# A first stage of block products: q and k of the band and B's gates are projected ahead of phase A and pass through DRAM

## The chip, the cores and the metric

The kernel runs on one core of a Trainium2 chip. The metric is the device time of one execution in microseconds (us). The two versions of the kernel are compared by the medians of several executions, and one execution of each is profiled.

The engines are TensorE (PE, with its weight loads PEld), VectorE (DVE), ScalarE (ACT), GpSimd (POOL) and SyncE (SP), which issues most of the loads. ACT issues most of the stores.

## The reference

The reference is one step of a hybrid encoder layer over 1024 prompt frames and 8 x 16 sample frames, 1152 columns in all, with a model width of 1024, all in float32:

```
z   = x @ w_in -> [q_A | k_A | v_A | q_B k_B v_B | q_C | gate logits (3*D) | a_B | b_B]
o_A = chunk-band softmax attention over the own chunk and the 8 before (16 heads of 64)
o_B = gated DeltaNet: causal conv + SiLU, normalised q/k, delta rule (8 heads of 128)
o_C = cross-attention into 256 memory tokens (4 heads of 256)
h   = LayerNorm(alpha * x + (sum_b sigmoid(gate_b) * o_b) @ w_out)
y   = LayerNorm(alpha * h + relu(h @ w_ff1 + b_ff1)^2 @ w_ff2 + b_ff2)
```

The keys and values of the band are outputs as well, among others.

## The kernel before

**Products.** A float32 product is made of three matmuls on halves: a matrix is split into `hi` (rounded to the type float32r) and `lo` (the rest), and hi\*hi, hi\*lo and lo\*hi are added in PSUM. x lies in SBUF transposed, as `xh` and `xl`, eight blocks of 128 rows by 1152 columns. The columns of `w_in` are cut into 80 tiles of 128: q of the band is tiles 0 to 7, k 8 to 15, v 16 to 23, the conv inputs of B 24 to 47, q of C 48 to 55, the gates of A, B and C 56 to 79. `projected` makes one tile: three chunks of 384 columns, for each 8 x 3 matmuls into one of two PSUM banks (tag `g`), and after each chunk an evacuation that its caller hands in. One tile is 72 matmuls of 384 columns.

**Seven products of eight.** `ffn1` already has another form for most of its tiles. It takes two tiles of the weights, the two halves of the inner dimension and the two halves of the columns as a 2 x 2 x 2 block product and makes it from seven products in place of eight, with sums of blocks (`S`, made once from the right-hand side, and `tsum`, made for each pair from the weights). Each product has two banks of 288 columns with 12 matmuls each, so a pair of tiles is 168 matmuls of 288 columns.

**Stages.** The stages are phase A (band attention, and the conv front of B), phase C, phase B (the delta rule), the output projection and the two FFN products. Each opens pools of SBUF and PSUM, and the next one's pools take the same places.

**Phase A.** At its start x is loaded and split, q and k of group 0 are projected as x arrives, `b_setup` prepares B, and `a_v(0)` projects v. Then there are eight groups g of two heads. A group is eight units `a_prompt` (256 query rows of one head: S on PE, softmax over DVE, ACT and POOL, transposes, split, product with v into `od`), `a_sample`, a gate tile of B, `b_front` (three conv tiles of B: conv, SiLU, transposes, stores to DRAM) and then `a_qk(g + 1)` and `a_v(g + 1)`.

**What sets the order.** Nobody writes the engines' orders out. A scheduler goes through the program by priority, which is the order of the program text, and puts an instruction on its engine as soon as its inputs and a buffer are there. So a projection fills PE's gaps in attention code that stands ahead of it in the text. A tile named with a tag shares that tag's few buffers: `y` has four (the conv's working tile, the v copies, a copy in `a_qk`), `qs0`, `qs1`, `kd0`, `kd1` and `vv` have one each, `tb` (tag `t`) has two, `od` one, the tag `f` for conv and v transposes one.

**B's gates** are eight tiles. Seven are projected in phase A (`b_gate(1, g)` for g < 7), and the eighth, (1, 7), stands in the list `gates`, which the later stages use as filling work. All eight are stored to DRAM in `gb` and read by phase B.

Of the kernel before, what the change touches and what calls it, by code (L numbers as in the profile page):

```python
# [63 lines left out]
class K:  # L64
# [66 lines left out]
    def setup(self):  # L131
# [93 lines left out]
    def load_x(self, pool):  # L225
# [3 lines left out]
        for c in range(NCH):  # L229
# [3 lines left out]
            for k in range(KT):  # L233
                xr = pool.tile([P, (CW, 640, CW, 3 + CW)[k % 4]], F32, name=("e", "pt", "y", "z")[k % 4], bufs=(2, 2, 4, 2)[k % 4])[:, 0:CW]
                self.xlast = nc.sync.dma_start(xr, xT[c, :, k, :]).ins.name
                self.split(self.xh[:, k, n], self.xl[:, k, n], xr, "act")


    def phase_a(self, keep, pool, ps):
        nc, d = self.nc, self.d  # L240
        self.A = A = {}
        self.load_x(pool)
# [27 lines left out]
        for g in range(8):  # L270
# [11 lines left out]
            if g < 7:  # L282
                self.a_qk(g + 1, pool)
                self.a_v(g + 1, pool, ps)

    def a_qk(self, g, pool):
# [21 lines left out]
        def ev_k(c, p):  # L308
# [959 lines left out]
    def ffn1(self, pool, ps, hm, raws):  # L1268
# [7 lines left out]
        one, two = slice(0, H), slice(H, NT)  # L1276
        top, low = slice(0, 4), slice(4, 8)

        S = {i: tuple(pool.tile([P, 4, H], F32R, name=f"s{i}{n}") for n in "hl") for i in (2, 1, 4)}
        S[3] = hh[:, top, two], hl[:, top, two]  # L1280
        names = cycle("gtogto")

        def bank():
            tag = next(names)
            if tag == "g":
                return self.psg.tile([P, 512], F32, name="ps", tag="g")[:, 0:288]
            return ps.tile([P, 512], F32, name=tag + "p", tag=tag, bufs={"t": 2, "o": 3}[tag])[:, 0:288]

        def hidden(r, f, i):
            nc.scalar.activation(r, r, AF.Relu, bias=bf[:, f:f + 1])  # L1290
            nc.scalar.activation(r, r, AF.Square)
            nc.scalar.dma_start(self.hid[f, i], r)

        res = lambda: pool.tile([P, H], F32, name="r", bufs=3)
        for f in range(4):
            w = self.weights(d["w_ff1"][f].rearrange("p (k c) -> p k c", k=KT))
            for i in range(2):
# [7 lines left out]
                nc.scalar.dma_start(self.hid[f, i], r)  # L1305
        for k in range(4):
# [9 lines left out]
        pool = self.on_right("p2r")  # L1316
        A11, A12, A22 = [(hh[:, q, n], hl[:, q, n]) for q, n in ((top, one), (low, one), (low, two))]
        for f in range(4, NF, 2):
            R = {}
            for g in range(2):  # L1320
                src = d["w_ff1"][f + g].rearrange("p (k c) -> p k c", k=KT)
                for q in range(2):
                    R[q, g] = raws().rearrange("p (k c) -> p k c", k=4)
                    nc.sync.dma_start(R[q, g], src[:, 4 * q:4 * q + 4, :])
            t1, t2, t3, t4 = (pool.tile([P, 4, P], F32, name="tsum", bufs=6) for _ in range(4))
            half = lambda j: slice(288 * j, 288 * j + 288)
            keep = lambda: pool.tile([P, H], F32, name="keep", bufs=5)
            def product(a, raw):

                w = [self.wp.tile([P, 4, P], F32R, name=n, tag=n, bufs=4) for n in ("whi", "wlo")]  # L1330
                self.split(*w, raw)
                banks = []
                for j in range(2):
                    banks.append(bank())
                    for k in range(4):
                        for m, (x, y) in enumerate(((0, 0), (0, 1), (1, 0))):
                            self.mm(banks[j], lhsT=w[x][:, k, :], rhs=a[y][:, k, half(j)], start=k == m == 0, stop=k == 3 and m == 2)
                return banks

            def add(x, banks):  # L1340
                y = keep()
                for j in range(2):
                    nc.vector.tensor_add(y[:, half(j)], banks[j], x[:, half(j)])  # L1343
                return y

            p1 = keep()
            for j, b in enumerate(product(A11, R[0, 0])):
                nc.scalar.copy(p1[:, half(j)], b)
            hidden(add(p1, product(A12, R[1, 0])), f, 0)
            nc.gpsimd.tensor_sub(t1, R[0, 1], R[0, 0])  # L1350
            nc.gpsimd.tensor_sub(t2, R[1, 1], t1)
            u2 = add(p1, product(S[2], t2))
            u4 = add(u2, product(S[1], t1))
            nc.gpsimd.tensor_sub(t4, R[1, 0], t2)
            u5 = add(u2, product(A22, t4))
            nc.gpsimd.tensor_sub(t3, R[1, 1], R[0, 1])
            hidden(add(u4, product(S[4], R[1, 1])), f + 1, 0)
            b = product(S[3], t3)
            hidden(add(u5, b), f, 1)
            hidden(add(u4, b), f + 1, 1)  # L1360

# [167 lines left out]
```

## Time and profile before

| | us |
|---|---|
| median of 3 runs (lowest, highest) | 2717.9 (2714.59, 2720.93) |
| the profiled execution, time | 2710.72 |
| the profiled execution, span from first to last instruction | 2708.9 |
| PE busy | 2607.6 (96%) |
| DVE busy | 1494.4 (55%) |
| ACT busy | 1063.6 (39%) |
| POOL busy | 866.9 (32%) |

An engine is busy while an instruction of its runs; issuing a DMA is not counted. Matmuls overlap their successors, so a PE that is busy all the time can still hold matmuls of different pace. The mean granted TensorE clock is 0.987 of full speed.

### The profile page before, as it was taken

The page shows a single profiled execution, that of the slowest core. Times are in us where ns is not written, and L with a number is a line of the kernel's source. Part 1 is how long each engine was busy: PE and PEld are TensorE (multiplying, and loading weights), DVE is VectorE, ACT ScalarE, POOL GpSimd, SP SyncE. Part 2 cuts the span into 40 slices and gives each one's busy share as a digit, 9 for nine tenths or more (in the row PEclk, how much of TensorE's full clock was granted, in tenths as well). Part 3 has the DMA queues.
Part 4 walks back from the last instruction along what each step waited for, and adds up shares of the span by engine and source line. Part 5 has one row for each costly group of instructions (what it writes and reads, how often), then busy time and mean ns, then how long its engine had stood idle before and what let it go on. Part 6 is the DMA issues. An engine that isn't in the chain of part 4 may idle for free.

```text
span 2708.9 us, 46387 instructions
## 1 busy us (share of the span) xinstructions
PE 2607.6 (96%) x16793; PEld 2418.9 (89%) x16793; DVE 1494.4 (55%) x3475; ACT 1063.6 (39%) x2851; POOL 866.9 (32%) x1203
## 2 busy tenths in 40 slices
PE   8999999999999989999989999999999998999998
PEld 7989999999999989888978888888899997878887
DVE  5647474756556573333466666554644445544545
ACT  5646474646556462232433333233622223101103
POOL 2222222222222221221555555332354442231112
PEclk9999999999999999999999999899999999999999
DMA  6343434444343444444776767554322224522311
GB/s 224 109 148 120 149 119 161 137 149 146 128 160 116 149 147 150 148 146 159 243 196 199 205 204 205 177 174 155 114 104 100 100 100 150 202 66 74 125 41 70
DMA packets 283782, 390.57 MB, mean 144 GB/s; under 512 B 57232, under 2 KB 189984, under 8 KB 280992
## 3 DMA queue, kind: packets, MB, share of 16 engines
q1 hardware_dynamic: 211344, 269.53, 31.7%
q10 hardware_dynamic: 72208, 118.06, 12.5%
q8 instruction: 133, 2.18, 0.3%
q14 instruction: 97, 0.79, 0.1%
HBM read 291.28 MB, written 128.72 MB: 155 GB/s over the span
## 4 chain that ended last, share of the span: by engine, by line
PE 78%; DMA 9%; DVE 6%; issue 3%; ACT 1%; POOL 1%; SPq 0%; DVEq 0%; ACTq 0%; POOLq 0%
PE ps L115 38%; PE op L115 19%; PE tp L115 4%; PE od L115 3%; PE S L115 3%; PE t L115 2%; PE tb L120 2%; PE sc L115 1%; DVE tmp L788 1%; PE tp L120 1%; PE kk L115 1%; DMA bv<-spn 1%; PE o L115 1%; DMA wraw<-in_w_mem 1%; DMA uraw<-hid 1%
## 5 line engine op out<-in xcount | busy, mean ns | idle before, releaser
L115 PE MATMUL ps<-xh,whi 128*128 128x384 f32 (+2 forms) x2144 | 749.0, 349 | 10.3 <-POOL whi L170 7.4
L115 PE MATMUL ps<-xh,wlo 128*128 128x384 f32 (+2 forms) x2144 | 726.7, 339 | 1.4 <-DVE wlo L171 1.4
L115 PE MATMUL ps<-xl,whi 128*128 128x384 f32 (+2 forms) x2144 | 725.8, 339 | 0.0
L115 PEld LDWEIGHTS ps<-xh,whi 128*128 128x128 f32 (+1 forms) x2144 | 404.2, 189 | 22.7 <-POOL whi L170 7.6
L115 PEld LDWEIGHTS ps<-xl,whi 128*128 128x128 f32 (+1 forms) x2144 | 404.4, 189 | 9.0 <-issue 5.0
L115 PEld LDWEIGHTS ps<-xh,wlo 128*128 128x128 f32 (+1 forms) x2144 | 403.5, 188 | 6.8 <-issue 2.5
L170 POOL TENSOR_SCALAR whi<-wraw 128x512 fp32r<-128x512 f32 x205 | 138.4, 676 | 441.6 <-PE ps L115 361.3
L115 PE MATMUL op<-l,xh 128*128 128x512 f32 x576 | 225.7, 392 | 8.0 <-DVE l L171 8.0
L115 PE MATMUL op<-h,xh 128*128 128x512 f32 x576 | 225.2, 394 | 8.3 <-POOL h L170 4.7
L115 PE MATMUL op<-h,xl 128*128 128x512 f32 x576 | 225.4, 391 | 0.0
L171 DVE TENSOR_TENSOR wlo<-wraw,whi 128x512 fp32r<-128x512 f32 x205 | 146.7, 717 | 137.4 <-POOL whi L170 134.1
L374 POOL TENSOR_SCALAR pt<-pt,sta 128x640 f32<-128x640 f32 (+3 forms) x144 | 110.9, 770 | 277.5 <-DVE sta L373 230.0
L166 ACT CAST xh<-uraw 128x384 fp32r<-128x384 f32 x96 | 45.5, 512 | 293.7 <-PE op L115 195.5
L620 DVE SCALAR_TENSOR_TENSOR y<-z,wc,y 128x384 f32<-128x384 f32 (+1 forms) x216 | 132.8, 615 | 28.4 <-ACT y L617 18.8
L170 POOL TENSOR_SCALAR h<-raw 128x512 fp32r<-128x512 f32 x64 | 54.3, 870 | 276.6 <-DVE acc L1412 168.0
L1412 DVE TENSOR_TENSOR acc<-op,acc 128x512 f32<-128x512 f32 x108 | 73.7, 688 | 117.4 <-PE op L115 117.4
L115 PEld LDWEIGHTS op<-h,xh 128*128 128x128 f32 x576 | 109.0, 189 | 33.0 <-POOL h L170 5.7
L115 PEld LDWEIGHTS op<-l,xh 128*128 128x128 f32 x576 | 109.1, 189 | 31.5 <-DVE l L171 8.7
L115 PEld LDWEIGHTS op<-h,xl 128*128 128x128 f32 x576 | 109.0, 189 | 22.7
L372 ACT ACTIVATE pt<-pt,sta 128x640 f32<-128x640 f32 (+3 forms) x144 | 101.0, 701 | 64.3 <-DVE sta L371 53.4
L1290 ACT ACTIVATE keep<-keep,bf 128x576 f32<-128x576 f32 x56 | 42.0, 774 | 211.2 <-DVE keep L1343 211.2
L370 DVE CUSTOM_DVE_ANT_0 pt<-S,tab 128x640 f32<-128x640 f32 (+4 forms) x128 | 83.8, 655 | 52.4 <-PE S L115 38.7
(473 smaller groups left out, 5971.7 us busy)
## 6 DMA issues: line engine op xcount, KB each, us to landing
wraw<-in_w_in SPq DMA_DIRECT2D x160, 256.0 KB
raw<-in_w_ff SPq DMA_DIRECT2D x120, 256.0 KB
uraw<-hid SPq DMA_DIRECT2D x32, 576.0 KB
kb<-in_cak SPq DMA_DIRECT2D x16, 1024.0 KB
vb<-in_cav SPq DMA_DIRECT2D x16, 1024.0 KB
hid<-keep ACTq DMA_DIRECT2D x56, 288.0 KB
o_aks<-in_cak ACTq DMA_DIRECT2D x32, 496.0 KB
o_avs<-in_cav ACTq DMA_DIRECT2D x32, 496.0 KB
```

The costliest lines, as they stand in the source:

```text
L115: ins = self.nc.tensor.matmul(out, **kw)
L120: ins = self.nc.tensor.transpose(out, **kw)
L166: nc.scalar.copy(hi, raw)
L170: nc.gpsimd.tensor_scalar(hi, raw, 1.0, 0.0, op0=ALU.mult, op1=ALU.add)
L171: nc.vector.tensor_sub(lo, raw, hi.bitcast(F32))
L370: nc.vector.tensor_tensor_reduce(out=P_, in0=S, in1=tab, scale=1.0, scalar=-3e38, op0=ALU.add, op1=ALU.max, accum_out=st[:, 0:1])
L372: nc.scalar.activation(P_, P_, AF.Exp, bias=st[:, 1:2], accum_out=st[:, 2:3])
L374: nc.gpsimd.tensor_scalar(P_, P_, st[:, 3:4], 0.0, op0=ALU.mult, op1=ALU.add)
L620: nc.vector.scalar_tensor_tensor(y[:, :w], z[:, i:i + w], wc[:, i:i + 1], y[:, :w], op0=ALU.mult, op1=ALU.add)
L788: nc.vector.tensor_tensor(tmp[:, 0:t, 0:t], y[:, 0:t, 0:t], m[:, 0:t, t].unsqueeze(1).broadcast_to([72, t, t]), op=ALU.mult)
L1290: nc.scalar.activation(r, r, AF.Relu, bias=bf[:, f:f + 1])
L1412: nc.vector.tensor_add(a, o, a)
```

## The change

A stage `phase_0` goes ahead of phase A, with pools of its own. It loads x into one large tile `xm`, projects q and k of groups 0 and 1 in the old way (tiles 0, 8, 1 and 9), makes the block sums of x, and then runs ten pairs through `seven`, the body of the loop of `ffn1` made into a function: six pairs (q, k) of groups 2 to 7 and four pairs of B's gates. The sixteen tiles of q and k go to a new DRAM array `zqk`, the gates to `gb` as before.

`a_qk` no longer projects. It loads six chunks of 128 x 384 from `zqk` into tiles of the tag `y` and hands them to the old evacuations, which now read SBUF. It stands ahead of `b_front(g)` in the text, no longer behind it. The gate tile leaves phase A's loop, and (1, 7) leaves the list `gates`. `seven` holds, for each pair, four weight loads, four sums of weights on POOL, seven products of 2 x 12 matmuls, fourteen evacuations and four calls of `out`; its text is the loop of `ffn1` shown above. `ffn1` calls the same new functions and computes what it did.

```
             self.right = st.enter_context(ExitStack())
+            with self.pools("0", "p0") as (pool, ps):
+                self.phase_0(pool, ps)
             with self.pools("a", "pa") as (pool, ps):
...
-        self.gates = [(0, 0), (0, 1), (0, 2), (0, 3), (1, 7)] + [(2, t) for t in range(4)] + [(a, t) for t in range(4, KT) for a in (0, 2)]
+        self.gates = [(0, 0), (0, 1), (0, 2), (0, 3)] + [(2, t) for t in range(4)] + [(a, t) for t in range(4, KT) for a in (0, 2)]
...
+        self.zqk = self.dram.tile([16, P, NT], F32, name="zqk")
...
+    def phase_0(self, pool, ps):
+        nc, d = self.nc, self.d
+        xm = self.on_right("xm").tile([P, KT, NT], F32, name="xm")
+        raw = lambda: pool.tile([P, 512], F32, name="raw", bufs=6)
+        S = self.block_tiles(pool, True)
+        self.load_x(xm)
+        w_in = lambda t: d["w_in"][t].rearrange("p (k c) -> p k c", k=KT)
+        def plain(t):
+            def ev(c, p):
+                r = raw()[:, 0:CW]
+                nc.scalar.copy(r, p)
+                nc.scalar.dma_start(self.zqk[t][:, c * CW:(c + 1) * CW], r)
+            return ev
+        both = [self.projected(t, plain(t), w) for t, w in zip((0, 8), self.first)]
+        for f in both * NCH:
+            run(f, KT)
+        for f in both:
+            run(f)
+        for t in (1, 9):
+            self.project(t, plain(t))
+        self.block_sums(S, xm)
+        right = self.on_right("p0r")
+        bank = self.rotate(ps)
+        half = lambda i: slice(i * NT // 2, (i + 1) * NT // 2)
+        for g in range(2, 8):
+            def store(r, i, j):
+                nc.scalar.dma_start(self.zqk[8 * i + g][:, half(j)], r)
+            self.seven([w_in(g), w_in(8 + g)], S, raw, right, bank, store)
+        for g in range(0, 8, 2):
+            def gate(r, i, j):
+                self.sigmoid(r, r, r)
+                nc.scalar.dma_start(self.gb[g + i][:, half(j)], r)
+            self.seven([w_in(64 + g), w_in(65 + g)], S, raw, right, bank, gate)
+        self.right.close()
     def phase_a(self, keep, pool, ps):
...
-        self.load_x(pool)
...
             if g < 7:
                 run(self.a_sample(g, pool, ps))
-                run(self.b_gate(1, g, pool))
+                self.a_qk(g + 1, pool)
             self.b_front(g, pool, ps)
...
             if g < 7:
-                self.a_qk(g + 1, pool)
                 self.a_v(g + 1, pool, ps)
...
             if c > 0:
-                y = pool.tile([P, CW], F32, name="y", bufs=4)
-                nc.scalar.copy(y, p)
+                y = p
...
-        if g:
-            self.project(g, ev_q)
-            self.project(8 + g, ev_k)
-        else:
-            both = [self.projected(t, ev, w) for t, ev, w in zip((0, 8), (ev_q, ev_k), self.first)]
-            for f in both * NCH:
-                run(f, KT)
-            for f in both:
-                run(f)
+        for t, ev in ((g, ev_q), (8 + g, ev_k)):
+            for c in range(NCH):
+                z = pool.tile([P, CW], F32, name="y", bufs=4)
+                nc.sync.dma_start(z, self.zqk[t][:, c * CW:(c + 1) * CW])
+                ev(c, z)
...
+    def seven(self, srcs, S, raws, pool, bank, out):
+        (the body of the loop of ffn1: four weight loads, four sums of weights on POOL,
+         seven products of 2 x 12 matmuls of 288 columns, fourteen evacuations, four calls of out)
```

## Rows read from the trace of the kernel before

**Rows 1.** The page, parts 1 and 4: busy us of the engines; the chain's shares.

```profile
PE 2607.6 (96%) x16793; PEld 2418.9 (89%) x16793; DVE 1494.4 (55%) x3475; ACT 1063.6 (39%) x2851; POOL 866.9 (32%) x1203
...
PE 78%; DMA 9%; DVE 6%; issue 3%; ACT 1%; POOL 1%; SPq 0%; DVEq 0%; ACTq 0%; POOLq 0%
```

**Rows 2.** Busy time by stretch, two groups of phase A; columns as named.

```profile
core 0: us, PE busy (x) PEld busy (x) DVE busy (x) ACT busy (x) POOL busy (x), PEclk, DMA share, GB/s
490.60:612.87 122.27, 122.27 (x834) 118.42 (x834) 74.74 (x201) 69.14 (x195) 31.74 (x62) 1.00 0.42 141
612.87:735.14 122.27, 122.27 (x834) 118.43 (x834) 74.71 (x201) 69.15 (x195) 31.73 (x62) 1.00 0.42 141
```

**Rows 3.** The chain of waits: start, us, what (384 columns, then 288).

```profile
1043.78 23.92 PE ps L115 x136
...
1974.73 1.58 PE tp L115 x12
1976.32 1.60 PE op L115 x12
```

**Rows 4.** Block sums of `ffn1`: count, ns min/median/max, first and last start.

```profile
L1365 DVE TENSOR_TENSOR s2l<-hm,s2h x4: 743/744/748, 1946.5 to 1953.8; 128x576 fp32r<-128x576 f32 x4
...
L1364 ACT CAST s2h<-hm x4: 667/675/676, 1942.9 to 1948.9; 128x576 fp32r<-128x576 f32 x4
```

**Rows 5.** Busy time by stretch at the start.

```profile
0.00:10.00 10.00, 1.46 (x3) 0.96 (x4) 4.05 (x11) 5.27 (x10) 7.12 (x24) 1.00 0.77 259
20.00:30.00 10.00, 8.40 (x48) 8.18 (x48) 5.64 (x11) 3.54 (x8) 2.05 (x5) 1.00 0.95 287
```

**Rows 6.** ACT, then PE, at the start: `b_setup`'s last chunk, the first `od`.

```profile
54.38 0.57 ACT L545 ACTIVATE e<-ps,par 8x384 f32<-8x384 f32 x1 [0.68 <-DVE e L550]
...
90.08 0.28 PE L115 MATMUL od<-pth,vv 128*128 128x256 f32 x1
```

**Rows 7.** PE in order of time, group 7: the first matmul of five units' `od`.

```profile
947.30 0.28 PE L115 MATMUL od<-pth,vv 128*128 128x256 f32 x1
...
993.05 0.41 PE L115 MATMUL od<-pth,vv 128*128 128x256 f32 x1
...
1000.45 0.28 PE L115 MATMUL od<-pth,vv 128*128 128x256 f32 x1
...
1005.89 0.39 PE L115 MATMUL od<-pth,vv 128*128 128x256 f32 x1 [0.74 <-DVE ptl L424]
...
1014.00 0.37 PE L115 MATMUL od<-pth,vv 128*128 128x256 f32 x1
```

**Rows 8.** PE, then ACT, in order of time: group's last S, next group's first `qs`.

```profile
523.63 0.31 PE L115 MATMUL S<-kd,qs 128*128 128x320 f32 x1
...
520.85 0.48 ACT L301 ACTIVATE qs<-ps 64x384 fp32r<-64x384 f32 x1
524.41 0.49 ACT L301 ACTIVATE qs<-ps 64x384 fp32r<-64x384 f32 x1
```

**Rows 9.** DVE, ACT and PE in order of time: `b_front`'s transpose among the sample's.

```profile
501.45 0.17 DVE L662 SCALAR_TENSOR_TENSOR rk<-rk,be 128x9 f32<-128x9 f32 x1
...
540.95 0.58 ACT L472 COPY pts<-tb 128x512 f32<-128x512 f32 x1
...
550.06 0.27 PE L120 MATMUL tb<-cst,os__5723 128*128 128x128 f32 x1
...
562.56 0.27 PE L120 MATMUL tb<-cst,rk 128*9 128x128 f32 x1
```

**Rows 10.** ACT in order of time, group 7: first and last of nine `z` copies.

```profile
940.23 0.48 ACT L610 COPY z<-ps 128x384 f32<-128x384 f32 x1 [2.13 <-PE ps L115]
...
986.23 0.47 ACT L610 COPY z<-ps 128x384 f32<-128x384 f32 x1
```

**Rows 11.** ACT in order of time, group 0: a conv chunk, first copy to store.

```profile
87.35 0.48 ACT L610 COPY z<-ps 128x384 f32<-128x384 f32 x1
...
96.40 0.33 ACTq L641 DMA_DIRECT2D spk<-y  x1
```

**Rows 12.** Busy time by stretch where filling work had run out (groups 0, 7).

```profile
150.00:160.00 10.00, 7.99 (x38) 6.98 (x38) 6.09 (x17) 4.26 (x10) 0.85 (x2) 0.72 0.17 48
...
990.00:1000.00 10.00, 6.90 (x40) 6.16 (x41) 7.91 (x24) 7.30 (x22) 1.60 (x2) 0.83 0.56 180
```

**Rows 13.** Busy time by stretch in phase B; ACT, the last gate's last chunk.

```profile
1700.00:1800.00 100.00, 93.76 (x692) 88.20 (x691) 51.95 (x142) 28.95 (x116) 37.44 (x41) 0.93 0.54 164
...
1802.49 0.49 ACT L220 ACTIVATE e<-ps 128x384 f32<-128x384 f32 x1 [0.35 <-PE ps L115]
```

More of the change, by code (lines that the diff above doesn't have):

```diff
@@ L223, in sigmoid, with load_x @@
         nc.scalar.activation(out, tmp, AF.Exp, scale=-1.0)
-    def load_x(self, pool):
+    def load_x(self, xm):
         nc = self.nc
@@ L233, in load_x @@
             for k in range(KT):
-                xr = pool.tile([P, (CW, 640, CW, 3 + CW)[k % 4]], F32, name=("e", "pt", "y", "z")[k % 4], bufs=(2, 2, 4, 2)[k % 4])[:, 0:CW]
+                xr = xm[:, k, n]
                 self.xlast = nc.sync.dma_start(xr, xT[c, :, k, :]).ins.name
                 self.split(self.xh[:, k, n], self.xl[:, k, n], xr, "act")
+    def phase_0(self, pool, ps):
[32 more added lines that the diff above has]
+        self.right.close()
     def phase_a(self, keep, pool, ps):
@@ L1275, in ffn1 @@
         nc.sync.dma_start(bf, d["b_ff1"])
[L1276 to L1292, printed above, removed]
+        S = self.block_tiles(pool)
+        bank = self.rotate(ps)
         res = lambda: pool.tile([P, H], F32, name="r", bufs=3)
+        ff1 = lambda f: d["w_ff1"][f].rearrange("p (k c) -> p k c", k=KT)
         for f in range(4):
-            w = self.weights(d["w_ff1"][f].rearrange("p (k c) -> p k c", k=KT))
+            w = self.weights(ff1(f))
             for i in range(2):
@@ L1305, in ffn1, with hidden, rotate, bank @@
                 nc.scalar.dma_start(self.hid[f, i], r)
+        self.block_sums(S, hm)
+        pool = self.on_right("p2r")
+        for f in range(4, NF, 2):
+            def hidden(r, g, i):
+                nc.scalar.activation(r, r, AF.Relu, bias=bf[:, f + g:f + g + 1])
+                nc.scalar.activation(r, r, AF.Square)
+                nc.scalar.dma_start(self.hid[f + g, i], r)
+            self.seven([ff1(f), ff1(f + 1)], S, raws, pool, bank, hidden)
+    def rotate(self, ps):
+        names = cycle("gtogto")
+        def bank(n=288):
+            tag = next(names)
+            if tag == "g":
+                return self.psg.tile([P, 512], F32, name="ps", tag="g")[:, 0:n]
+            return ps.tile([P, 512], F32, name=tag + "p", tag=tag, bufs={"t": 2, "o": 3}[tag])[:, 0:n]
+        return bank
+    def block_tiles(self, pool, all_=False):
+        S = {i: tuple(pool.tile([P, 4, NT // 2], F32R, name=f"s{i}{n}") for n in "hl") for i in (2, 1, 4, 3)[:3 + all_]}
+        if not all_:
+            S[3] = self.xh[:, 0:4, NT // 2:NT], self.xl[:, 0:4, NT // 2:NT]
+        return S
+    def block_sums(self, S, hm):
+        nc = self.nc
+        one, two = slice(0, NT // 2), slice(NT // 2, NT)
         for k in range(4):
@@ L1315, in ffn1 @@
             self.cast(S[4], k, a12)
[L1316 to L1360, printed above, removed]
@@ new lines, in seven, with product, add @@
+    def seven(self, srcs, S, raws, pool, bank, out):
+        nc = self.nc
+        H = NT // 2
+        A11, A12, A22 = [tuple(t[:, q, n] for t in (self.xh, self.xl)) for q, n in ((slice(0, 4), slice(0, H)), (slice(4, 8), slice(0, H)), (slice(4, 8), slice(H, NT)))]
+        R = {}
+        for g, src in enumerate(srcs):
+            for q in range(2):
+                R[q, g] = raws().rearrange("p (k c) -> p k c", k=4)
+                nc.sync.dma_start(R[q, g], src[:, 4 * q:4 * q + 4, :])
+        t1, t2, t3, t4 = (pool.tile([P, 4, P], F32, name="tsum", bufs=6) for _ in range(4))
+        half = lambda j: slice(288 * j, 288 * j + 288)
+        keep = lambda: pool.tile([P, H], F32, name="keep", bufs=5)
+        def product(a, raw):
+            w = [self.wp.tile([P, 4, P], F32R, name=n, tag=n, bufs=4) for n in ("whi", "wlo")]
+            self.split(*w, raw)
+            banks = []
+            for j in range(2):
+                banks.append(bank())
+                for k in range(4):
+                    for m, (x, y) in enumerate(((0, 0), (0, 1), (1, 0))):
+                        self.mm(banks[j], lhsT=w[x][:, k, :], rhs=a[y][:, k, half(j)], start=k == m == 0, stop=k == 3 and m == 2)
+            return banks
+        def add(x, banks):
+            y = keep()
+            for j in range(2):
+                nc.vector.tensor_add(y[:, half(j)], banks[j], x[:, half(j)])
+            return y
+        p1 = keep()
+        for j, b in enumerate(product(A11, R[0, 0])):
+            nc.scalar.copy(p1[:, half(j)], b)
+        out(add(p1, product(A12, R[1, 0])), 0, 0)
+        nc.gpsimd.tensor_sub(t1, R[0, 1], R[0, 0])
+        nc.gpsimd.tensor_sub(t2, R[1, 1], t1)
+        u2 = add(p1, product(S[2], t2))
+        u4 = add(u2, product(S[1], t1))
+        nc.gpsimd.tensor_sub(t4, R[1, 0], t2)
+        u5 = add(u2, product(A22, t4))
+        nc.gpsimd.tensor_sub(t3, R[1, 1], R[0, 1])
+        out(add(u4, product(S[4], R[1, 1])), 1, 0)
+        b = product(S[3], t3)
+        out(add(u5, b), 0, 1)
+        out(add(u4, b), 1, 1)
```

## The prediction

> **What bounds the kernel now.** I read the page first. PE is busy 96% of the span, and the chain that ended last is 78% PE [rows 1]. The kernel is a sum of PE's work wherever PE is fed, so the question is where the moved work lies and what it covers there. So I went on to the busy times by stretch. In phase A a group of two heads comes back every 122.27 us, and in it PE is never idle, while DVE is busy 74.7 us and ACT 69.1 [rows 2]. A full period is thus set by PE's count of matmuls. But DVE and ACT are not far: against a period shortened by a third they would be near full too.
>
> Then the chain's pieces for the pace. 136 matmuls of 384 columns take 23.92 us, 0.176 us each; 12 of 288 take 1.58 to 1.60, 0.1325 us each [rows 3]. A plain tile is 72 x 0.176 = 12.7 us, a pair 25.4. A pair by seven products is 168 x 0.1325 = 22.3 us.
>
> **The change, part by part.**
>
> *The products themselves.* Ten pairs save 25.4 - 22.3 = 3.1 us each, 31 us in all. This is the whole gain: everything else moves work or adds to it. The Trainium skill (TensorE: Matmul & The Clock Gate, "Wait — 56ns, not 53.3ns?") gives a matmul its columns at 2.4 GHz and some 2.5 ns. By that page a pair would go from 23.4 to 20.6 us and the gain, an estimate, be 28 us; the rows show a larger surplus per matmul and decide.
>
> *Block sums.* 28 DVE passes of about 0.74 us and 16 ACT casts of 0.67 [rows 4] are 21 and 11 us. They lie under tiles 1 and 9 (25.4 us of PE) and the first two products of the first pair, which need no sum. I take 0; without that cover up to 10 us.
>
> *The load of x* is as before: 10 us before PE has work, and some 2 us lost later [rows 5]. So phase 0 ends at 10 + 2 + 4 x 12.7 + 10 x 22.3 = 286 us. Its stores (9.4 MB to `zqk`) ride ACT's queue behind copies; nobody waits for them before phase A.
>
> *The start of phase A.* `b_setup` now begins at 286. Its projection costs 12.7 us, and from its last chunk to the first product with v there is a chain: 54.38 to 90.08, 35.7 us [rows 6]. Before, v(0), a gate tile and two conv chunks filled PE in that time. Now the gate is gone, so PE idles some 13 us there; if the chain can be shortened or hoisted, none. I count it in full: the first `od` comes at 286 + 12.7 + 35.7 = 334 instead of 90. **+244**.
>
> *The seven periods from the first `od` of group 0 to that of group 7.* Before they took 947.30 - 90.08 = 857 us [rows 6, 7]. Fourteen tiles of q and k and six gates leave them, 254 us, so PE's work alone gives (857 - 254) / 7 = 86.2 us a period. Whether it becomes 86.2 is the crux, because of a wait the change adds. The loads of a_qk(g+1) take tiles of the tag `y`, of which there are four, and stand ahead of `b_front(g)`. Six loads, ready at any time, take all four early in group g. They are released only when `qs` and `kd` of the next group are written, and these have one buffer each: the first write of `qs0` came at 520.85, that of `qs1` at 524.41, right behind the group's last S at 523.63 [rows 8]. Behind the loads, in the text, come the nine `y` of the conv. Are buffers given out in the order of the text? The transpose of `rk` in `b_front` says yes: its input was written at 501.45, both buffers of its tag were free from about 541.5 (the copy at 540.95) to 550.06, and it ran at 562.56, behind the sample's last, which stands ahead of it [rows 9]. So `b_front(g)` can put only two chunks into PSUM (tag `g`) while attention g runs, and the rest waits for its end; v(g+1) shares `y`, `g` and `f` and comes behind `b_front(g)`, and the next `od` waits for v. Filling work and attention no longer overlap as they do now.
>
> A period is then two stretches. Attention with little filling: units came 7.4, 5.4 and 8.1 us apart when filling had run out, mean 7.0 [rows 7]. For the three short units that follow a group's first I estimate 5. From the first `od` to the last S, about six pitches less 1.6, that is 3 x 5 + 3 x 7 - 1.6 = 34 us. Then `b_front` with the sample and v. Beside four units its nine chunks took 46 us from first to last [rows 10], 5.75 a chunk; PE alone would need 4.2 a chunk. Seven chunks at 4.2 to 5.75 are 30 to 40; to that come the start (3), the last chunk's chain (9.05 us from first copy to store [rows 11]) and the transposes and split of v (3): 45 to 55, and ACT and DVE have to carry the tail of attention and the sample beside it. I take 58, period 92. The ends: 86.2 (PE's own work, nothing excludes it) and 103 (the competition of [rows 10] in both stretches). Seven periods: 7 x 92 - 857 = **-213**.
>
> *The clock.* Where filling had run out for some 20 us, the granted clock of 10 us fell to 0.72 and 0.83 [rows 12], that is, part of it at 1.2 GHz. Each such stretch costs 10 x 0.17 to 10 x 0.28, 1.7 to 2.8 us of PE time. I put it into the 92. The Trainium skill (same page, "What's actually happening") says that idleness, not load, throttles the array, which is what these rows show; by it a period with a bare stretch pays again and again, and the sum would hold one such cost a period, some 12 to 20 us.
>
> *Loads from DRAM.* Four of six are there long before they are used; the last two wait for a buffer first, under PE's two waiting conv chunks. 0; without the cover about 3 us a period.
>
> *Evacuations* of q and k read SBUF in place of PSUM, and a copy of 0.48 us falls away twice a group: 0.
>
> *Group 7* has no `a_qk` behind it and runs as before, but its first two conv chunks were already done: 0 to 8.5, I take **+4**.
>
> *Phase B* has one gate tile less to fill with. Filling lasts to its end, and PE is busy 94% there [rows 13], so the gain is 0 to 12.7; I take **-6**.
>
> The sum is 244 - 213 + 4 - 6 = +29 us on the profiled execution's 2710.7 (span 2708.9 and 1.8 around it), 2740. The median of the runs is 7.2 above that execution, so the median forecast is 2747.
>
> **The rivals.** About 0.2% (5.4 us) is what a measurement of this kernel can tell from no change. The point of balance is a period of (857 - 242) / 7 = 87.9.
>
> 1. *The forecast*: filling and attention fall apart, period 89 to 97. Against it: even then PE has most of its work in each stretch. 2726 to 2782. Chance 0.47.
> 2. *Filling still flows beside attention* (the loads don't hold back the conv, or the two stretches are both full): 86.2 a period, -254, and with the other terms -12, or -23 with all of B's gain and no lag: 2695 to 2706. For it: in group 7 nine chunks and four units ran side by side with PE full [rows 7, 10]. Against it: [rows 8, 9]. It decides from a period under 87. Chance 0.27.
> 3. *No change*: period 87.2 to 88.7, within 5.4 us. Chance 0.12.
> 4. *Worse than the forecast*: ACT and DVE, near full, stretch both parts, period 97 to 103: +64 to +106, 2782 to 2824. Chance 0.14.
>
> **How the numbers follow.** The prediction is case 1's. The range reaches down into case 2 and up to most of case 4: 2692 to 2812; the likeliest case alone is 2726 to 2782. Faster 0.27, same 0.12, slower 0.61.
>
> **What would show it.** Phase 0: twelve matmuls of 288 columns in 1.6 us and its end near 286. The first `od` near 334. The distance between equal points of neighbouring groups: 92, against 122.27; PE's idle time in phase A, none before, near 6 us a group, ended by DVE or ACT. The `z` copies of `b_front(g)` in a block behind the last S of group g, not among its units. It is wrong if `z` copies run among the units or PE stays full at 86; the sum is also off if phase 0 is longer (sums late, boundary).

## The result and the profile after

| | before | after |
|---|---|---|
| median of the runs, us | 2719.4 (2714.6 to 2721.5) | 2871.4 (2868.7 to 2882.0) |
| profiled execution, us | 2710.7 | 2882.0 |
| granted clock, mean | 0.987 | 0.964 |

The ratio is 1.0581, 95% interval [1.0556, 1.0605]: 152 us slower, where 29 slower was forecast. The direction was right; the time lies 59 us above the upper end of the range. The two profiled executions stand 171 us apart (after's was 10.6 above its median, before's 8.7 below its own), and the terms below are measured between these two.

The page of the changed kernel, parts 1 and 4, answers to [rows 1].

```profile
PE 2665.0 (93%) x17033; PEld 2433.3 (84%) x17033; DVE 1606.8 (56%) x3665; ACT 1083.2 (38%) x2859; POOL 963.4 (33%) x1277
...
PE 71%; DMA 11%; DVE 8%; issue 4%; ACT 2%; POOL 2%; SPq 0%; ACTq 0%; DVEq 0%; POOLq 0%
```

PE still has the most work, but its share of the chain fell from 78% to 71%: DMA, DVE, ACT and POOL now hold it up here and there. Where, the view of busy time by stretch shows. `otmp` is ACT's copy out of a unit's finished `od`; the first one of a group marks its beginning. First come the seven periods from the first `otmp` of group 0 to that of group 7 as one stretch, then group 3 and group 4, each cut where the sample's first S runs, some 3 us behind the last S of the units at 705.05 and 811.34 (columns as in [rows 2]).

```profile
361.51:1099.81 738.30, 655.25 (x4327) 586.14 (x4327) 490.18 (x1354) 457.86 (x1277) 210.90 (x395) 0.96 0.46 153
675.57:708.00 32.43, 23.21 (x150) 17.66 (x152) 24.20 (x73) 21.62 (x55) 8.21 (x12) 1.00 0.35 118
708.00:778.88 70.88, 68.11 (x473) 63.86 (x465) 45.23 (x114) 42.54 (x123) 22.86 (x43) 0.98 0.52 175
778.88:814.00 35.12, 25.49 (x146) 19.25 (x146) 25.12 (x80) 22.73 (x59) 9.00 (x13) 0.95 0.33 109
814.00:886.57 72.57, 68.76 (x479) 63.57 (x478) 45.26 (x118) 44.56 (x130) 20.92 (x43) 1.00 0.54 175
```

A period is 738.30 / 7 = 105.5 us, against 122.3 before [rows 2] and 92 forecast. It has two parts, as forecast. In the first (32 to 35 us, or 29 to 32 up to the last S itself; forecast 34) attention runs alone, and PE works 23 of 32 us. In the second (71 to 73 us, or 74 to 75 from the last S; forecast 58) PE is busy for 68 of 71: full. What it does there is in the groups of PE's instructions in 708.00:778.88 (count, busy us, mean ns, idle before):

```profile
L117 PE MATMUL ps<-xh,whi 128*128 128x384 f32 x96 | 33.4, 348 | 0.0
L117 PE MATMUL ps<-xl,whi 128*128 128x384 f32 x96 | 33.2, 346 | 0.0
L117 PE MATMUL ps<-xh,wlo 128*128 128x384 f32 x96 | 32.8, 341 | 0.0
```

That is 288 matmuls of a projection, twelve chunks of 24: all nine of the conv and all three of v, 288 x 0.176 = 50.7 us at the pace of [rows 3]. (Matmuls overlap in the pipeline, so their busy times add up to more.) In 675.57:708.00 the same view has not one such matmul. ACT in order of time shows the order of the chunks: seven copies of `z` (the first and the last stand here), three of v, the first chunks of the next conv, and then the next group's first unit.

```profile
718.65 0.46 ACT L646 COPY z<-ps 128x384 f32<-128x384 f32 x1
...
753.78 0.48 ACT L646 COPY z<-ps 128x384 f32<-128x384 f32 x1 [0.32 <-PE ps L117]
759.47 0.46 ACT L379 COPY y<-ps 128x384 f32<-128x384 f32 x1
...
767.65 0.49 ACT L379 COPY y<-ps 128x384 f32<-128x384 f32 x1 [2.17 <-PE ps L117]
772.65 0.46 ACT L646 COPY z<-ps 128x384 f32<-128x384 f32 x1
...
777.67 0.48 ACT L646 COPY z<-ps 128x384 f32<-128x384 f32 x1
...
778.88 0.37 ACT L468 COPY otmp<-od 64x256 f32<-64x256 f32 x1 [0.35 <-PE od L117]
```

Before, the nine copies ran among the units [rows 10]. The first stage is as forecast: the chain of waits in 100:130 has its pace (twelve matmuls of 288 columns a bank), and the stretch 50:250 is full.

```profile
99.92 1.58 PE op L117 x12
101.51 1.60 PE ps L117 x12
```

```profile
50.00:250.00 200.00, 200.00 (x1475) 200.00 (x1474) 99.38 (x180) 22.76 (x44) 94.56 (x101) 1.00 0.30 105
```

At the boundary to phase A something stands that wasn't in the forecast: the zero stores of `b_setup`. Here are the stretch 300:320, and then ACT, its queue and PE in order of time, to the first `otmp`.

```profile
300.00:320.00 20.00, 1.92 (x6) 1.30 (x6) 4.79 (x14) 3.77 (x9) 4.70 (x9) 0.55 0.97 317
```

```profile
306.24 13.99 ACTq L559 DMA_DIRECT2D dxy<-e  x9
...
320.85 0.48 ACT L589 ACTIVATE oT<-ps 8x384 f32<-8x384 f32 x1 [14.78 <-DMA dxy<-e]
321.38 0.58 PE L117 MATMUL ps<-xh,whi 128*64 128x384 f32 x1 [13.31 <-ACT oT L589]
...
361.51 0.37 ACT L468 COPY otmp<-od 64x256 f32<-64x256 f32 x1
```

With these stores ahead of it, ACT's next eviction is 14.8 us late, and PE waits 13.3 us for its PSUM bank. (The 13.99 us run from the first issue to the end of the ninth; the issues themselves are short, as the last section shows.) Before, the first `otmp` came at 91.05 (its product at 90.08 [rows 6]).

Phase B as one stretch, from the last store of `oc` to the last of `og`, before and then after:

```profile
1309.89:1828.34 518.45, 473.32 (x3287) 437.71 (x3286) 323.28 (x853) 177.10 (x621) 269.03 (x317) 0.96 0.69 201
```

```profile
1462.87:2005.71 542.84, 488.92 (x3269) 450.51 (x3268) 320.54 (x852) 171.58 (x612) 267.70 (x316) 0.93 0.65 191
```

It is 24.4 us longer. PE's busy time times the granted clock is the same, 454 and 455 us: 15.6 us of the growth are the same work at a lower clock, 8.8 are idle time. Each of the two is one execution. In eight more kernels below whose phase B has the same text as the changed one's, without (1, 7) and with the same rate of filling, this stretch took 530.7 to 559.8 us, so a single profile gives it to some 15 us only.

| term, us | forecast | measured |
|---|---|---|
| first `od` or `otmp` of group 0 | +244 | 361.5 - 91.05 = +270.5 |
| seven periods | -213 | 738.3 - 856.9 = -118.6 |
| group 7 to its end | +4 | 98.97 - 96.34 = +2.6 |
| phase B | -6 | +24.4 |
| phase C and all behind B | 0 | -1.5 and -6.1 |
| sum | +29 | +171 |

### The profile page after: what moved, and what is told of

Its sections match the earlier page's. It is cut to its first block, busy times and chain, and to the rows that moved or that the text cites. A ratio compares the mean times of both kernels' runs of the same rounds, so it can differ in the third digit from the quotient of the medians.

```text
span 2880.2 us, 47545 instructions
## 1 busy us (share of the span) xinstructions
PE 2665.0 (93%) x17033; PEld 2433.3 (84%) x17033; DVE 1606.8 (56%) x3665; ACT 1083.2 (38%) x2859; POOL 963.4 (33%) x1277
## 4 chain that ended last, share of the span: by engine, by line
PE 71%; DMA 11%; DVE 8%; issue 4%; ACT 2%; POOL 2%; SPq 0%; ACTq 0%; DVEq 0%; POOLq 0%
PE ps L117 29%; PE op L117 21%; PE tp L117 6%; PE t L117 3%; PE S L117 2%; PE od L117 2%; DMA bv<-spn 2%; PE tb L122 2%; DMA kb<-in_cak 2%; DVE pt L406 2%; PE sc L117 1%; PE kk L117 1%; PE tp L122 1%; DVE ptl L455 1%; PE o L117 1%
## 5 line engine op out<-in xcount | busy, mean ns | idle before, releaser
L117 PE MATMUL ps<-xh,whi 128*128 128x384 f32 (+2 forms) x1748 | 612.6, 350 | 31.0 <-ACT oT L589 13.5
L117 PE MATMUL ps<-xh,wlo 128*128 128x384 f32 (+2 forms) x1748 | 591.8, 339 | 0.0
L117 PE MATMUL ps<-xl,whi 128*128 128x384 f32 (+2 forms) x1748 | 591.2, 338 | 0.0
L117 PEld LDWEIGHTS ps<-xh,whi 128*128 128x128 f32 (+1 forms) x1748 | 333.9, 191 | 42.7 <-ACT oT L589 13.8
L117 PEld LDWEIGHTS ps<-xl,whi 128*128 128x128 f32 (+1 forms) x1748 | 334.1, 191 | 5.2 <-issue 2.1
L117 PEld LDWEIGHTS ps<-xh,wlo 128*128 128x128 f32 (+1 forms) x1748 | 333.0, 190 | 5.4 <-issue 3.1
L173 POOL TENSOR_SCALAR whi<-wraw 128x512 fp32r<-128x512 f32 x165 | 117.3, 712 | 373.5 <-PE ps L117 279.0
L174 DVE TENSOR_TENSOR wlo<-wraw,whi 128x512 fp32r<-128x512 f32 x165 | 119.3, 725 | 137.5 <-POOL whi L173 131.4
```

The source lines that it names most:

```text
L117: ins = self.nc.tensor.matmul(out, **kw)
L173: nc.gpsimd.tensor_scalar(hi, raw, 1.0, 0.0, op0=ALU.mult, op1=ALU.add)
L174: nc.vector.tensor_sub(lo, raw, hi.bitcast(F32))
```

## The experiments

Two theories were there to begin with. Theory 1: the loads of q and k hold the four `y` ahead of the conv (the forecast's mechanism). Its rival: with 36 us less PE work a period, phase A is set by its own chains, whatever holds the conv. Theory 2 came with the counts above: behind the last S PE is full, with twelve chunks where the forecast had counted seven. "Seven periods" below is from the first `otmp` of group 0 to that of group 7. Differences between two kernels are taken between their ratios to the kernel before, as not all ran on one chip.

**A tag of their own for the loads.**

```diff
-                z = pool.tile([P, CW], F32, name="y", bufs=4)
+                z = pool.tile([P, CW], F32, name="zq", bufs=5)
...
-            vb = pool.tile([P, 4, 4, P], F32, name="vb", bufs=2)
+            vb = pool.tile([P, 4, 4, P], F32, name="vb", bufs=1)
```

> The loads of q and k get a tag of their own with five buffers; the room comes from the second buffer of the sample's values (vb). Theory 1 (the loads hold the four y ahead of the conv, so filling and attention fall apart): the z copies of b_front stand among the units again, the period goes from 105.5 to 88 to 94, and the time falls by 80 to 120 us, to 2750 to 2790. Rival (phase A has too little PE work left to cover its own chains, whatever the buffers): period 103 to 107, time 2850 to 2890. Rival (the order of the writes of qs and kd on ACT and DVE holds the conv, not the tag): as the first rival, with the z copies still in a block.

Measured: 2832.5 us, ratio 1.0417 [1.0387, 1.0447]; seven periods 692.0, 98.9 each. Group 4 in this kernel, cut where the last S of its units is done: busy time by stretch, then projection matmuls in its first part.

```profile
771.10:828.93 57.83, 54.25 (x342) 51.58 (x341) 42.78 (x111) 37.05 (x105) 17.41 (x31) 1.00 0.35 115
828.93:867.03 38.10, 31.17 (x251) 26.29 (x249) 24.75 (x74) 23.82 (x66) 11.13 (x23) 0.91 0.69 240
```

```profile
L117 PE MATMUL ps<-xh,whi 128*128 128x384 f32 x64 | 22.5, 351 | 1.7 <-ACT y L653 1.7
L117 PE MATMUL ps<-xl,whi 128*128 128x384 f32 x64 | 22.0, 344 | 0.0
L117 PE MATMUL ps<-xh,wlo 128*128 128x384 f32 x64 | 21.9, 342 | 0.0
```

192 projection matmuls, eight chunks, now run beside the units, where there were none. So the tag did hold the conv. But the first part grows from 32 to 35 us to 58, the second shrinks from 72 to 38, where PE is now bare (31 of 38 us, clock 0.91): 46 us gained over seven periods, where theory 1 had 80 or more, and 13 of them are lost again ahead of the periods, as the first `otmp` comes at 374.7. Period and time lie between the two theories. The forecast's mechanism holds, and its rival is half right: undoing it is not enough.

**The loads behind `b_front` in the text.**

```diff
-                self.a_qk(g + 1, pool)
             self.b_front(g, pool, ps)
+            if g < 7:
+                self.a_qk(g + 1, pool)
```

> Tags as in the changed kernel, but a_qk(g+1) stands behind b_front(g) in the text. Theory 1: the conv's y come first, its chunks run beside the units, the period is 88 to 98 (the loads and writes of q and k now wait for the conv's last y), time 2760 to 2820. Rival (too little PE work to cover the chains): period 105 or more, since the loads now come late too: 2870 to 2900.

Measured: 2833.3 us, ratio 1.0411 [1.0372, 1.0449]; seven periods 694.9, 99.3 each. The tag and the place in the text are two ways to the same 43 to 46 us in the periods (the first `otmp` is 11 us later here). Both expectations missed: the period lies 1.3 us above the first one's 88 to 98, the time 13 above its range, and both are below the rival's.

**The zero stores in the first stage.**

```diff
-                    nc.scalar.dma_start(self.matrices(self.dxy[i][j], 3 * c, 3), ...)
...
+            if g == 3:
...
+                            nc.sync.dma_start(self.matrices(self.dxy[i][j], 3 * c, 3), ...)
```

> The twelve zero stores of b_setup go into the first stage, on SP's queue, behind the second pair. If they cost what the trace shows (ACT held 14.6 us, PE idle 13.3 us at 321), the first otmp comes at 346 to 349 in place of 361.5 and the time falls by 12 to 15 us, to 2857. Rival (another chain of b_setup ends at about the same time): 0 to 5 us.

Measured: 2863.2 us, ratio 1.0529 [1.0498, 1.0561]. The first `otmp` of this kernel (ACT in order of time), and its stretch 300:320:

```profile
339.92 0.37 ACT L475 COPY otmp<-od 64x256 f32<-64x256 f32 x1
```

```profile
300.00:320.00 20.00, 16.49 (x88) 14.91 (x89) 10.12 (x28) 15.07 (x32) 6.13 (x12) 0.91 0.71 245
```

21.6 us earlier, more than the wait itself and than the 12 to 15 expected: the stretch of 20 us with PE at 1.92 us and 0.55 of the clock is gone. Of this some 8 (medians) to 14 us (ratios) reach the end; in the profiled execution the seven periods were 19.6 us longer (757.9, mean clock 0.94 against 0.96), for which nothing in the edit gives a reason.

**Gate (1, 7) back in phase B.**

```diff
-        self.gates = [(0, 0), (0, 1), (0, 2), (0, 3)] + ...
+        self.gates = [(0, 0), (0, 1), (0, 2), (0, 3), (1, 7)] + ...
```

> The gate tile (1,7) is put back into phase B's list, and so computed twice: 12.7 us more of PE work, and the value stored in gb is that of the plain projection. If phase B grew by 24 us because its filling ran out 45 us before its end (and because its first filling tile now waits for loads), B falls from 543 to 520 to 532 us and the time by 10 to 23. Rival (B is longer because of a lower clock, or PE is its bound): the time stays or rises by up to 13 us.

Measured: 2868.4 us, ratio 1.0557 [1.0522, 1.0593], no difference in time that can be told. B took 527.1 us in place of 542.8:

```profile
1468.89:1996.03 527.14, 478.81 (x3291) 442.07 (x3290) 319.65 (x853) 177.34 (x621) 270.19 (x318) 0.95 0.68 198
```

The text of phase B and its counts show why a tile more or less changes little: when the gate tiles run out, `fills` goes on with the first matmuls of the output projection. One of their six groups in B, in the kernel before and in the changed one:

```profile
L115 PE MATMUL ps<-hi,xh 128*128 128x512 f32 x11 | 4.7, 428 | 0.0
L117 PE MATMUL ps<-hi,xh 128*128 128x512 f32 x20 | 9.2, 459 | 0.0
```

All six are 67 matmuls of 512 columns before, 121 in the changed kernel and 71 here, so that B holds 3287, 3269 and 3291 matmuls. What runs there early is missing behind B: from the last store of `og` to the end it took 880.6, 874.5 and 882.5 us. So 8 us of this experiment's gain in B come back behind it, and phase A was 4 us longer.

**A second buffer for `kb`.** The chain of waits of group 3 in the changed kernel had a new piece, the late load of the sample's keys:

```profile
709.17 12.05 DMA kb<-in_cak
721.35 0.65 PE S L117 x6
722.00 2.86 PE od L117 x12
```

```diff
-            kb = pool.tile([P, 4, 528], F32, name="kb", bufs=1)
+            kb = pool.tile([P, 4, 528], F32, name="kb", bufs=2)
...
-            vb = pool.tile([P, 4, 4, P], F32, name="vb", bufs=2)
+            vb = pool.tile([P, 4, 4, P], F32, name="vb", bufs=1)
```

> The sample's keys (kb) get a second buffer, the values (vb) give theirs up; all else as the changed kernel. Rival that the late load of kb is the new bound (12.05 us of it in the chain of a period, and it stands ahead of the last unit's od): the second unit's product and all behind it come 8 to 12 us earlier, period 94 to 98, time 2815 to 2835. Theory 2 (behind the last S PE is full with seven chunks of b_front and the three of v, which the forecast of 58 left out): kb costs only the start of that stretch, 2 to 5 us a period, time 2835 to 2860.

Measured: 2874.4 us, ratio 1.0598 [1.0572, 1.0624]; seven periods 738.9, 105.6 each. Nothing gained, less than either expectation: 12 us in the chain of a period, and worth nothing. PE's waits for `kb` in these periods, four of 4.4 us in all in the changed kernel, are gone, and nothing waits for `vb`; but PE has the same twelve chunks to do.

**The gates as filling again.** (`e7_own_and_gates` adds the tag of `e1_own_tiles`; `e8_setup_early` also puts `b_setup` behind the fourth pair of the first stage, with the zero stores on SP's queue.)

```diff
-        for g in range(0, 8, 2):
...
-            self.seven([w_in(64 + g), w_in(65 + g)], S, raw, right, bank, gate)
...
                 run(self.a_sample(g, pool, ps))
+                run(self.b_gate(1, g, pool))
...
+            if g == 5:
+                self.b_setup(keep, right, ps)
```

> Only q and k stay in the first stage; the eight gates of B go back to where they were as plain tiles, seven as filling in phase A and (1,7) in phase B. The first stage ends 89 us earlier. Theory 2 (the attention stretch is bare, PE idle or slow for a third of its 35 us, so there is room for a gate's 12.7 us): the period grows by 1 to 5 us only, from 105.5 to 106 to 111, B shrinks by 10 to 16 as when (1,7) was put back, and the time is 2765 to 2810. Rival (the place of a tile in the text decides, and the gate runs behind the sample, one after the other with b_front): period 116 to 119, time 2845 to 2870.

> The tag of their own for the loads of q and k (five buffers, vb with one) and the gates as filling, together. PE's own work is 98.7 us a period. Theory 1 and 2 together (the conv flows among the units, and what e1 still had bare is filled): period 100 to 104, time 2735 to 2770. Rival (the attention's own chain and the sample set some 10 us a period that no filling covers): period 108 to 112, time 2790 to 2825.

> As e7_own_and_gates, and b_setup (projection, its chain of exponentials and transposes, the zero stores on SP's queue) stands in the first stage, between the pairs. If the boundary costs what the changed kernel's profile shows (291 to 361: 70 us, of which 34 are PE's own work), the first otmp comes 35 to 45 us earlier than without it, at 240 to 250, and the time is 35 to 45 below that of e7_own_and_gates: 2695 to 2735, at or a little below the kernel before. Rival (PE takes its work in the order of the text, so the chain of b_setup stops the products of the first stage for its 36 us): 0 to 10 below.

| | us | ratio, interval | first `otmp` | a period | B |
|---|---|---|---|---|---|
| `e6_gates_fill` | 2859.1 | 1.0538 [1.0504, 1.0572] | 280.7 | 114.6 | 529.2 |
| `e7_own_and_gates` | 2789.5 | 1.0283 [1.0260, 1.0307] | 282.4 | 106.7 | 531.4 |
| `e8_setup_early` | 2767.9 | 1.0195 [1.0166, 1.0223] | 251.0 | 108.4 | 531.7 |

With the loads on `y` a gate's 12.7 us cost 9.1 a period; the period lies between the two expectations, the time is the rival's: mostly one after the other. With their own tag they cost 7.8 (106.7 against 98.9); the period lies between the two expectations, the time at the rival's lower end. `b_setup` in the first stage brings the first `otmp` 31 us forward, a little under the 35 to 45 expected, and some 24 us of it reach the end; the time of 2695 to 2735 was missed, as it started from the one expected for `e7_own_and_gates`.

**A lower rate of filling in phase B.** (`FILL` is the number of filling steps taken behind each step of phase B's streams.)

```diff
-FILL0, FILL = 5, 1.35
+FILL0, FILL = 5, 1.25
```

> The changed kernel with one constant: phase B takes 1.25 filling steps in place of 1.35 behind each step of its streams. If B's 24 us came from filling that runs out before its end, B falls from 543 to 522 to 535 us and the time by 8 to 20, to 2851 to 2863. Rival (B's growth comes from its beginning, where its first filling tile now waits for loads, or from the clock): 0 to 3 us.

Measured: 2889.4 us, ratio 1.0618 [1.0577, 1.0660], B 551.0 us at a clock of 0.92. Both expectations missed: the time rose by some 10 us, with intervals that overlap. B lies within the 531 to 560 us of the kernels with the old rate, and in the pair below the lower rate has the shorter B, so nothing here says what the rate does to B; that filling which runs out early makes B longer is not borne out.

**Only the gates by seven products.** (`e11_gates_and_rate` is the same with FILL at 1.25.)

```diff
-        for t in (1, 9):
-            self.project(t, plain(t))
+        for t in range(2):
+            self.project(64 + t, gate_ev(t))
...
+            if g:
+                self.project(t, ev)
+                continue
```

> The other half of the change: q and k of groups 1 to 7 are projected in phase A as before the change, the gates go out of it. The first stage holds q and k of group 0 and gates 0 and 1 plain, the gates 2 to 7 as three pairs, and b_setup as in e8_setup_early; a_qk stands behind b_front. PE's own work is 109.6 us a period. Theory 2 (attention needs the two tiles of q and k as cover; a gate less is within what it can spare): period 110 to 113, first otmp 180 to 195, B 530 to 540, time 2710 to 2745. Rival (any tile taken out of phase A leaves the chains as they are): period 117 to 122, time 2765 to 2800.

> As e10_gates_seven, with 1.25 filling steps in phase B: what e9_fill_rate gains against the changed kernel (8 to 20 us by the first theory there, 0 to 3 by its rival), time 2695 to 2735.

Measured: 2781.7 us, 1.0216 [1.0180, 1.0253], and 2778.5 us, 1.0222 [1.0188, 1.0256]. The seven periods of the first of them:

```profile
195.17:991.60 796.43, 774.17 (x5283) 731.48 (x5282) 491.18 (x1361) 449.16 (x1281) 228.00 (x418) 0.99 0.43 141
```

113.8 a period for 109.6 us of PE work, PE busy for 97%: with q and k as cover phase A follows its filling closely, much as theory 2 has it (110 to 113, so just missed). The times missed (2710 to 2745 and 2695 to 2735), B taking 559.8 and 548.6 us where 530 to 540 was expected. The rate makes no difference that can be told, and this half of the change by itself doesn't pay either.

**v ahead of `b_front`.** (`e13_v_ahead_own` adds the tag of `e1_own_tiles`; `e14_all` is `e8_setup_early` with v ahead.)

```diff
                 self.a_qk(g + 1, pool)
+                nc.scalar.dma_start(self.oa[g], A["oT"])
+                self.a_v(g + 1, pool, ps)
             self.b_front(g, pool, ps)
```

> The changed kernel with a_v(g+1) ahead of b_front(g) in the text (and the store of oa before it). Theory 2 (behind the last S PE is full with seven chunks of b_front and then the three of v, so v's 13.8 us stand whole on the path to the next od): v follows the last S at once, the next od comes about 30 us behind it, b_front's chunks fall beside the next group's units, which were bare: period 90 to 97, time 2765 to 2815. Rival (the stretch behind the last S is set by the sample and the writes of q and k, not by the order of PE's work): period 102 to 108, time 2850 to 2890.

> e12_v_ahead and e1_own_tiles together. If the tag and the place of v are two ways out of the same wait, the gains do not add: period 90 to 97, time 2760 to 2800. If they are two waits, period 87 to 91, time 2735 to 2765.

> All that helped together: own tag, v ahead, gates as filling in phase A and (1,7) in B, b_setup in the first stage. e8_setup_early with v ahead. PE's own work is 98.7 us a period. If v's place is what kept e8's period at 108.4: period 99 to 103, time 2705 to 2735. If the sample and the last units set it: 106 to 110, 2755 to 2780.

Measured: 2877.3 us, 1.0589 [1.0565, 1.0614]; 2886.3 us, 1.0616 [1.0583, 1.0649]; 2813.2 us, 1.0348 [1.0330, 1.0366]. Periods 105.5, 103.1 and 111.6. Here theory 2, as it was put, is wrong. ACT in order of time in `e12_v_ahead`, a group whose last S came at 810:

```profile
842.41 0.38 ACT L390 CAST vv<-pvt 128x256 fp32r<-128x256 f32 x1
...
843.62 0.48 ACT L646 COPY z<-ps 128x384 f32<-128x384 f32 x1 [0.41 <-PE ps L117]
...
878.12 0.46 ACT L646 COPY z<-ps 128x384 f32<-128x384 f32 x1
886.12 0.37 ACT L468 COPY otmp<-od 64x256 f32<-64x256 f32 x1
```

v is ready at 843, 32 us behind the last S, and still the next `otmp` comes at 886: the conv's chunks took v's place before it. PE's busy time in the block is as it was (70.0 and 70.4 us in groups 3 and 4 of the changed kernel, counted from the last S):

```profile
810.60:886.12 75.52, 70.36 (x500) 65.61 (x500) 53.32 (x139) 47.71 (x141) 22.46 (x48) 1.00 0.50 158
```

So with `b_front` still ahead of the next group's units in the text, v's place does not shorten that part: the conv and v together fill it in either order. The other two lie above both of their expectations. Where v's place did matter, with the own tag (103.1 against 98.9) and in `e14_all` (111.6 against 108.4), it cost.

**Another first tile in phase B, and the same stage with plain projections.**

```diff
-        self.gates = [(0, 0), (0, 1), (0, 2), (0, 3)] + [(2, t) for t in range(4)] + ...
+        self.gates = [(0, t) for t in range(5)] + [(2, t) for t in range(5)] + ...
```

```diff
-            self.seven([w_in(g), w_in(8 + g)], S, raw, right, bank, store)
+            self.project(g, plain(g))
+            self.project(8 + g, plain(8 + g))
```

> The changed kernel with the list of gates in another order: phase B begins with (0, 4), which needs no earlier part of og, and all other tiles follow as they were. If B's growth of 24 us comes from its first filling tile waiting for loads behind phase C's stores, the first state is stored 7 us earlier and B falls to 525 to 535, time 2853 to 2863. Rival (it is the missing tile, as e4_gate_back showed 16 us with a tile more, or the clock): B 537 to 550, time within 8 us of the changed kernel's.

> The changed kernel with the ten pairs as plain projections in the same first stage, no products of blocks. The forecast's first term (22.3 against 25.4 us a pair): the first otmp comes 31 us later, at 392, and the time rises by 27 to 35 us, to 2898 to 2906. Rival (the products' evictions and sums hold PE up too, so the gain is less): 10 to 25 us.

Measured: 2878.3 us, 1.0610 [1.0576, 1.0644], with B at 535.7 and the first state stored at 1597.4, 130.5 us into B (1593.8 before the edit, 130.9 into B; 7 less was expected): the first tile is not the cause. B's length alone, between the two expectations, could not tell. And 2906.1 us, 1.0709 [1.0670, 1.0748]; its first `otmp`:

```profile
392.63 0.37 ACT L477 COPY otmp<-od 64x256 f32<-64x256 f32 x1
```

That is 31.1 us behind the changed kernel's, and the time is 35 us longer. The products bring what was forecast.

## Why the prediction was right in direction and wrong in size

**The products, -31: right.** 31.1 us by `e16_plain_stage`. The estimate from the Trainium skill (TensorE: Matmul & The Clock Gate, "Wait — 56ns, not 53.3ns?"), 28 us, is a little under it; the surplus per matmul that the rows showed decided rightly. Phase 0's last product ended at 291, forecast 286.

**The mechanism of phase A: right, and shown.** `z` copies in a block behind the last S, none among the units; with a tag of their own for the loads, or with the loads behind `b_front` in the text, a part of them runs among the units again. PE's idle time is 11.9 us a period, about twice the 6 that were named, and half of it waits for DVE's softmax.

**The step that failed: "b_front with the sample and v ... I take 58", and so the period of 92.** The attention part was 32 to 35 us, as forecast or a little less; the other 71 to 73, and that is the whole miss of 94 us over seven periods. The working counted seven chunks of the conv and for v only its transposes and split. The count of matmuls shows twelve chunks: v's projection (three, 12.7 us) was left out, and the two conv chunks that were to be done beside attention run ahead of it, in the same full stretch (8.4 us). Those are 21 us; the last chunk's chain of 9 us, which the forecast added, lies under v. The rows needed were there: PE's work of 86.2 a period less what attention itself needs, all put into one part.

**Rival 2 (86.2 if the filling flows) would have failed too.** In `e1_own_tiles` it flows, and the period is 98.9. What then sets it was not isolated: its profile shows PE bare at the end of each group, where the last units and the sample run with the filling used up. Before, the two tiles of q and k stood there and PE never waited [rows 2]. What leaves gives back less the more has left: the six gates of `e10_gates_seven` shortened the seven periods by 60.5 of 76 us, the twenty tiles of the changed kernel by 119 of 254, with a tag of their own by 165.

**The boundary, 334: too early by 26 to 27 us.** The forecast took `b_setup`'s chain from [rows 6], where the zero stores had been issued beside the load of x. Here they come between the loads of phase A and the chain. `e3_zeros_early` gives 21.6 of it back: from the end of the products, at 289.7 in that run, to the first `otmp` it takes 50.2 us, where the forecast had 48.4. The rest is mostly phase 0's later end, 291 for 286.

**The clock, "I put it into the 92": too small.** The mean over the seven periods is 0.96, against 1.00 before; 4% of 655 us of busy time is 26 us, an estimate of 3.7 a period, where 1.7 to 2.8 were taken. The rule of the Trainium skill (same page, "What's actually happening") that idleness throttles the array is borne out by 300:320, PE busy 1.92 of 20 us at 0.55.

**Phase B, -6: wrong in sign, +24, and the reason for it misread.** "Filling lasts to its end" was taken to mean that a tile less shortens B. The last gate's last chunk at 1802.49 [rows 13] was not the end of the filling: behind it come the first matmuls of the output projection, and more of them when a tile is missing (121 against 67). So B's work stays what it was, and the gain, 6.1 us, comes behind B: there the runs without (1, 7) took 871 to 878 us, those with it 881 to 882. In B itself the five runs with the tile took 526 to 532 us at clocks of 0.95 to 0.96, those without it 531 to 560 at 0.92 to 0.95, and the one profile of the kernel before 518. PE's busy time times the clock is 453 to 459 us in all of them. That B is longer because a less filled PE is granted less clock fits these rows, but was not tried by itself; the first tile does not explain it, and of the rate nothing can be told. Its cause is open.

**Group 7, +4:** measured +2.6.

No version here beats the kernel before. The best, `e8_setup_early`, is 2% slower.

## What to carry to other kernels

Before work is moved out of a stretch in which one engine is full, count what that stretch still has to cover: filling that leaves gives back its time only until the chains beside it are bare. Where two parts fall apart, give every instruction of the period to one of the parts and add each part up by counts from the trace; a list of what comes to mind forgets one (here a whole projection). And a piece of the chain is not a price: 12 us of a late load were worth nothing while the engine behind it had its work still to do.

## What was not expected of the hardware

ACT issued nothing but zero stores from 306.24 to 320.80, with the DMA engines at 0.97 of their time in 300:320 and 317 GB/s. Yet the issues themselves are short: the view of the tile `dxy` has all twelve at 0.37 to 0.87 us. Between them ACT stood still until earlier transfers had landed. The chain of waits has the first store of this batch in flight for 11.35 us, and the fifth goes out when it has landed:

```profile
306.24 11.35 DMA dxy<-e
317.59 0.02 issue
317.61 0.37 ACTq L559
```

Full DMA engines alone don't do this. In `e3_zeros_early` the same twelve stores went out on SP's queue within 8.7 us, at 0.38 to 1.32 us each, in a stretch where the DMA engines were no less full:

```profile
17.00:27.00 10.00, 10.00 (x59) 10.00 (x58) 9.85 (x13) 6.74 (x14) 4.61 (x3) 1.00 1.08 342
```

So here ACT paid little for the issues and much for the landings that a later issue in its order waited for, with its evictions behind them. And the bare stretch cost more than the wait that is seen in it: with PE at 1.92 of 20 us the granted clock was 0.55, a mixture of 1.2 and 2.4 GHz. From the end of the products to the first `otmp` the same 245 matmuls kept PE busy for 46.2 of 70.4 us at a clock of 0.81, and for 43.1 of 50.2 at 0.97 once the stall was gone: 17.0 us less idle time and 3.2 less busy time, where the wait itself was 13.3.
